# Differential attention with one transpose each for queries and keys, one square sum per half head, and the combination of the softmaxes put ahead of the next row maxima

## The chip, the cores and the metric

The kernel runs on one core of a Trainium2 chip. The metric is device time in microseconds (us) of one execution, as the median of several runs. The core has five engines that run side by side, each with its own queue of instructions: TensorE (PE in the profile; its weight loads, PEld, overlap its matmuls), VectorE (DVE), ScalarE (ACT), GpSimd (POOL) and SyncE (SP), which here only issues transfers between DRAM and on-chip memory. Instructions of different engines wait for one another by semaphores; an instruction that waits holds up everything behind it in its own queue.

## The reference

One decoder layer on 1024 tokens of width 1024: RMSNorm, one input projection, three branches (a chunkwise mLSTM, a causal differential attention, a cross-attention into 256 memory tokens), sigmoid gates, a projection, then a squared-ReLU MLP. The change touches the differential attention alone. It has 8 heads; each has two queries and two keys of width 64 (components 0 and 1) and one value of width 128:

```python
q = rms_norm(q, q_g)
k = rms_norm(k, k_g)
...
s = jnp.einsum('bhcqd,bhckd->bhcqk', qblk, kt).astype(jnp.float32) * scale
s = jnp.where(kpos[None, :] <= qpos[:, None], s, -jnp.inf)
p = jax.nn.softmax(s, axis=-1)
a = p[:, :, 0] - lam * p[:, :, 1]
return jnp.einsum('bhqk,bhkv->bhqv', a.astype(vt.dtype), vt)
```

All arithmetic is float32. The kernel feeds TensorE with a rounded format and so keeps each operand as a high part (the rounded value) and a low part (the rest), and multiplies high by high, high by low and low by high.

## The kernel before, in words

The stages run one after the other: the norm and cross-attention, the mLSTM, a stretch of gate matmuls, the differential attention (`branch_d`) with the remaining gate matmuls as filling, the gates that are still left, the merge (`tail`) and the MLP (`mlp`).

Inside `branch_d` the generator `d_gemm` projects the tokens. A half head (j, 0 to 15) is 512 tokens of one head, in four tiles of 128. A tile takes eight groups of three matmuls (`mm3`), and each `yield` hands control back after one group; `fill(n)` runs n groups, and gate matmuls once the projection is through. When a tile is done, `evict` copies it out of PSUM: the value v as high and low part (dv), the raw queries and keys (draw), and their squares (dscr). `rest`, which `after()` runs at the start of the next step, sums the squares, and for the fourth tile takes the inverse root on POOL (drr) and sets up `prep`, the list of evictions of this half head: `turns` gives transposes of draw (into a PSUM tile that the profile calls pr, the projection's other buffer), queries as qT (dq) and keys as kd and kl (dk, dkl: high and low part).

Before the change draw holds each 64-wide query or key twice side by side. A transpose of 128 x 128 then gives one component with two copies, one above the other on the partitions. In qT one copy stays the high part and the other becomes the low part, so that one matmul of depth 128 against the doubled kd gives high by high and low by high at once; a second matmul against kl adds the rest. Four groups of four transposes serve a half head, one group per step, each with its eviction; the scaling of the keys by their norm (`scale`) stands at the end of the second of these steps.

After eight tiles ahead of it, the main loop runs 64 steps (and five to drain). Step s is one block of 128 queries of head s // 8; its width is 128 x (s % 8 + 1) keys. "Step 0" to "step 7" below means s % 8. A step does, in this order: the scores of component 0 into sc, their row maxima with the mask (the custom VectorE instruction, `tmask`) and the exponential (dpe); `after()`; `combine(s - 1)`, which puts the two exponentials of the step before together; four groups of filling; `values(s - 2)`, the product with v (po) and its two-instruction eviction into doS, a high part on ScalarE and a low part on VectorE; the next entry of `prep`; a group; scores of component 1; the transposes of the combined rows (tp) into daT, high part on ScalarE and low part on VectorE, around the second exponential; three more groups; the second function of the `prep` entry; in between `norm`, in four parts, once in four steps. `ahead` splits the next head's projection weights (w) and asks for the ones after.

While this stage runs, `self.pinned` and `InOrder` make TensorE, VectorE and ScalarE keep the order in which the program was written. SP's queue and POOL's are ordered by the scheduler. Two score tiles, two projection tiles and two tp/po tiles exist in PSUM, and each is reused when its last reader is done.

## Time and profile before

| | |
|---|---|
| median of 3 runs | 2195.02 us (2193.86 to 2195.88) |
| the profiled execution | 2194.59 us, its span 2192.8 us, granted TensorE clock 0.999 |
| main loop's scores on TensorE | first at 646.8 us, last at 1122.6 us |
| transposes of draw (pr) | 256, first at 630.6 us, last at 1086.5 us |
| one head (eight steps) | 59.43 us from 819.82 to 879.25 |

An execution's own time is a little longer than its span. A group of the profile gives line, engine, operation, `written<-read`, then count and durations; in brackets stands the idle time of that engine just before and what ended it. All instructions of the three pinned engines have the line of the helper that records them (67, 92, 95), so the tile names tell them apart. In the table by stretches a row holds the length, then the busy time of PE, PEld, DVE, ACT and POOL with counts, the granted clock, and the transfers' share and rate.

### The profile page before, as it was taken

The numbers are of one execution on the slowest core, as the hardware profiler recorded it, in microseconds if no ns is written. First come the engines' busy times: TensorE is split into PE (matmuls) and PEld (weight loads), VectorE is DVE, ScalarE is ACT, GpSimd is POOL, SyncE is SP. The second block draws the span as 40 slices with busy tenths as digits, with TensorE's granted clock in tenths as the row PEclk, the third lists the DMA queues.
The fourth block names the chain that finished last, engine by engine and source line by source line (L and its number), as shares of the span: only waits on it lengthen the run. The fifth ranks groups of instructions, "written<-read, shape, count | busy, mean of one in ns | idle before, by whom it ended". The sixth has DMA issues, their size and how long they took to land.

```text
span 2192.8 us, 30563 instructions
## 1 busy us (share of the span) xinstructions
PE 2166.7 (99%) x11254; PEld 1874.8 (85%) x11254; DVE 1385.5 (63%) x2628; ACT 969.5 (44%) x1949; POOL 534.9 (24%) x709
## 2 busy tenths in 40 slices
PE   8999999999999999999999999999999999999998
PEld 6888789888899999999888888888878888788887
DVE  6455457554138888888753233454588778876678
ACT  7543445444246666666543111223433333543331
POOL 3210000000011111111100002101566667564444
PEclk9999999999999999999999999999999999999999
DMA  7032222201311111110135344435534454744442
GB/s 252 21 117 87 88 62 79 79 14 63 116 49 35 35 31 39 39 37 25 54 120 173 116 139 130 144 111 177 191 126 159 154 198 158 268 165 158 159 158 96
DMA packets 110947, 242.38 MB, mean 111 GB/s; under 512 B 10921, under 2 KB 19406, under 8 KB 108750
## 3 DMA queue, kind: packets, MB, share of 16 engines
q1 hardware_dynamic: 108494, 227.85, 31.4%
q10 hardware_dynamic: 2304, 12.58, 1.4%
q8 instruction: 88, 1.44, 0.3%
q14 instruction: 61, 0.50, 0.1%
HBM read 173.25 MB, written 67.14 MB: 110 GB/s over the span
## 4 chain that ended last, share of the span: by engine, by line
PE 77%; DVE 12%; ACT 4%; DMA 4%; issue 2%; POOL 1%; SPq 0%; ACTq 0%; POOLq 0%; DVEq 0%
PE mm L92 46%; PE p L92 21%; PE sc L92 4%; PE tp L95 2%; PE po L92 2%; DVE sc L67 1%; ACT dpe L67 1%; DVE dpe L67 1%; DMA raw<-in_wkv 1%; DVE wo L67 1%; DVE draw L67 1%; PE pr L95 1%; DVE dst L67 1%; DVE u L67 1%; POOL wraw L67 1%
## 5 line engine op out<-in xcount | busy, mean ns | idle before, releaser
L92 PE MATMUL mm<-hT,w 128*128 128x512 f32 x1920 | 464.2, 395 | 1.6 <-ACT gt L605 1.6
L92 PE MATMUL mm<-w,hT 128*128 128x384 f32 (+3 forms) x2496 | 454.6, 329 | 0.0
L92 PEld LDWEIGHTS mm<-hT,w 128*128 128x128 f32 x1920 | 353.5, 188 | 75.5 <-ACT gt L605 2.0
L92 PEld LDWEIGHTS mm<-w,hT 128*128 128x128 f32 x2496 | 388.2, 188 | 8.8
L67 POOL TENSOR_TENSOR wraw<-wraw 128x128 f32<-128x128 f32 x496 | 321.3, 672 | 171.3 <-DMA wraw<-in_wdown 127.6
L92 PE MATMUL p<-xo,wo 128*128 128x512 f32 x1344 | 307.6, 390 | 2.2 <-ACT u L67 0.7
L92 PE MATMUL p<-xd,wo 128*128 128x512 f32 x1344 | 305.7, 389 | 0.6 <-DVE acc L67 0.5
L92 PEld LDWEIGHTS p<-xo,wo 128*128 128x128 f32 x1344 | 251.3, 188 | 57.1 <-DVE u L67 2.3
L92 PEld LDWEIGHTS p<-xd,wo 128*128 128x128 f32 x1344 | 252.0, 188 | 54.1 <-DVE acc L67 1.0
L92 PE MATMUL mm<-kt,w 128*128 128x512 f32 x1152 | 261.3, 389 | 0.0
L92 PEld LDWEIGHTS mm<-kt,w 128*128 128x128 f32 x1152 | 216.3, 188 | 44.8
L67 ACT CAST wo<-wraw 128x896 fp32r<-128x896 f32 x125 | 116.5, 944 | 258.1 <-POOL wraw L67 119.7
L67 DVE TENSOR_TENSOR wo<-wraw,wo 128x896 fp32r<-128x896 f32 x125 | 155.7, 1254 | 111.6 <-ACT wo L67 109.6
L67 ACT ACTIVATE dpe<-sc,dst,drr 128x256 f32<-128x256 f32 (+7 forms) x128 | 106.7, 833 | 62.0 <-DVE dst L67 51.9
L116 ACT CAST w<-raw 128x256 fp32r<-128x256 f32 (+2 forms) x128 | 69.0, 567 | 126.6 <-PE mm L92 99.5
L117 DVE TENSOR_TENSOR w<-raw,w 128x256 fp32r<-128x256 f32 (+2 forms) x128 | 81.5, 664 | 41.7 <-ACT w L116 41.7
L67 DVE CUSTOM_DVE_ANT_0 sc<-sc,tmask 128x256 f32<-128x256 f32 (+7 forms) x128 | 96.9, 757 | 3.6 <-PE sc L92 2.4
L140 POOL TENSOR_SCALAR hss<-hss 128x4 f32<-128x4 f32 x8 | 3.5, 442 | 378.0 <-ACT mscr L907 378.0
L92 PE MATMUL mm<-mh,w 128*128 128x512 f32 x256 | 78.9, 389 | 0.0
L106 DVE TENSOR_TENSOR w<-raw,w 128x256 fp32r<-128x256 f32 (+1 forms) x64 | 27.1, 439 | 80.0 <-ACT w L105 79.4
L67 DVE TENSOR_TENSOR w<-raw,w 128x384 fp32r<-128x384 f32 (+2 forms) x112 | 65.8, 598 | 15.8 <-ACT w L67 15.6
L92 PEld LDWEIGHTS po<-dv,daT 128*128 128x128 f32 x576 | 74.8, 189 | 0.9
(325 smaller groups left out, 2947.2 us busy)
## 6 DMA issues: line engine op xcount, KB each, us to landing
wraw<-in_wup SPq DMA_DIRECT2D x64, 256.0 KB, 3.2
r_d<-xts SPq DMA_DIRECT2D x16, 1024.0 KB, 4.2
xd<-r_d SPq DMA_DIRECT2D x16, 1024.0 KB, 5.4
wraw<-in_wdown SPq DMA_DIRECT2D x64, 256.0 KB, 4.2
raw<-in_wgate SPq DMA_DIRECT2D x48, 256.0 KB, 3.1
gates<-gt SPq DMA_DIRECT2D x48, 256.0 KB, 2.1
raw<-in_wd SPq DMA_DIRECT2D x32, 384.0 KB, 3.1
kraw<-y SPq DMA_DIRECT2D x24, 512.0 KB, 4.6
```

The costliest lines, as they stand in the source:

```text
L67: return self.tc.keep_in_program_order(f(*a, **k))
L92: self.pin(self.nc.tensor.matmul(out, l, r, start=start, stop=stop))
L95: self.pin(self.nc.tensor.transpose(out, x, self.ident))
L106: low = lambda: self.V.tensor_sub(lo, src, f32(hi))
L116: nc.scalar.copy(hi, src)
L117: nc.vector.tensor_sub(lo, src, f32(hi))
L140: g.tensor_scalar(r, ss, 1.0 / width, EPS, op0=ALU.mult, op1=ALU.add)
```

## The change

Queries and keys: draw is one tile per half head, without doubling. One group of four transposes turns both queries of four token tiles, a second both keys; component 0 then lies on partitions 0 to 63 and component 1 on 64 to 127. The high parts are copied there, 64 partitions at a time. The query's low part goes to the other 64 partitions of the same component. The key's high part is brought to the other 64 partitions by two transfers from on-chip memory to on-chip memory on SP's queue (`twice`). The key's low part stays where it is, in one of four fixed tiles whose other half POOL fills with zero once. `prep` has three entries: queries with the key scaling behind them, keys, the transfers.

Square sum: one reduction over the four tiles of a half head in place of four; the squares of the four tiles have one tile.

Order: `scores` gives back the row maxima as a function (`top`). For component 0, `combine(s - 1)` now stands ahead of it, and `after()` behind the exponential. In the eight tiles ahead of the loop the first entry of `prep` comes two groups earlier.

On VectorE in step 7, from its first row maxima (ISA is the custom instruction) to the second, before:

```order
L67 ISA sc_9377,dst_9376<-sc_9377,tmask 128x1024
L67 ISA dst_9376 128x1
L67 SCALAR_TENSOR_TENSOR dst_9376<-dst_9376,drr_8363 128x1
L67 TENSOR_REDUCE drr_9107<-dscr_9372 128x4
L67 RECIPROCAL dst_9282<-dst_9282 128x2
L67 SCALAR_TENSOR_TENSOR dst_9282<-dst_9282,dv 128x1
L67 SCALAR_TENSOR_TENSOR dpe_9280<-dpe_9281,dst_9282,dpe_9280 128x896
L67 SCALAR_TENSOR_TENSOR doS_9323<-po_9402,dst_9187,doS_9323 128x128
L67 TENSOR_TENSOR doS_8965<-doS_8965,dso_9295 128x512
L67 TENSOR_TENSOR dkl_9103<-pr_9418,dk_9102 128x512
L67 ISA sc_9428,dst_9376<-sc_9428,tmask 128x1024
```

and now, from the combination:

```order
L67 RECIPROCAL dst_8412<-dst_8412 128x2
L67 SCALAR_TENSOR_TENSOR dst_8412<-dst_8412,dv 128x1
L67 SCALAR_TENSOR_TENSOR dpe_8410<-dpe_8411,dst_8412,dpe_8410 128x896
L67 ISA sc_8499,dst_8498<-sc_8499,tmask 128x1024
L67 ISA dst_8498 128x1
L67 SCALAR_TENSOR_TENSOR dst_8498<-dst_8498,drr_7537 128x1
L67 SCALAR_TENSOR_TENSOR doS_8452<-po_8523,dst_8322,doS_8452 128x128
L67 TENSOR_TENSOR doS_8115<-doS_8115,dso_8424 128x512
L67 ISA sc_8542,dst_8498<-sc_8542,tmask 128x1024
```

The combination (dpe) moved from behind the maxima to ahead of them; the square sum and the key's low part left this step; the low part of the value (doS) now follows the maxima at once.

On ScalarE in step 4, from the first exponential (dpe) to the second, before:

```order
L67 ACTIVATE dpe_9087,dst_9089<-sc_9090,dst_9089,drr_8363 128x640
L67 ACTIVATE doS_8965<-po_9121,dst_8934 128x128
L67 ACTIVATE dq_9101<-pr_9130,dv 128x512
L67 ACTIVATE yd_9145<-tp_9140,dv 128x512
L67 CAST daT_9160<-tp_9155 128x512
L67 CAST w_9164<-raw_8988 128x384
L67 ACTIVATE dpe_9088,dst_9089<-sc_9148,dst_9089,drr_8363 128x640
```

and now:

```order
L67 ACTIVATE dpe_8220,dst_8222<-sc_8223,dst_8222,drr_7537 128x640
L67 ACTIVATE doS_8115<-po_8255,dst_8085 128x128
L67 ACTIVATE dq_8237<-pr_8264,dv 64x512 x2
L67 ACTIVATE yd_8281<-tp_8276,dv 128x512
L67 CAST daT_8296<-tp_8291 128x512
L67 CAST w_8300<-raw_8133 128x384
L67 ACTIVATE dpe_8221,dst_8222<-sc_8284,dst_8222,drr_7537 128x640
```

Both query copies (dq), each 64 high, stand in this step where one stood; step 5 holds both key copies in the same way. The place of the exponential ahead of the value's high part (doS) is the old one.

On SP in the same stretch, weight loads (raw), an output store (y), before:

```order
L1018 DMA raw_8244<-in_wd 128x768
L1018 DMA raw_8418<-in_wd 128x768
L436 DMA y<-yd_8401 128x512
L1018 DMA raw_8698<-in_wd 128x768
L1018 DMA raw_8810<-in_wd 128x768
```

and now:

```order
L1018 DMA raw_8133<-in_wd 128x768
L1018 DMA raw_8298<-in_wd 128x768
L436 DMA y<-yd_8281 128x512
L1083 DMA dk_8238<-dk_8238 64x512 x2
L1018 DMA raw_8556<-in_wd 128x768
L1018 DMA raw_8669<-in_wd 128x768
```

The two doubling transfers (dk) stand behind the store of step 0 or 4 and ahead of the next weight loads.

The diff:

```diff
--- before.py
+++ after.py
@@ -1039,66 +1039,76 @@
         nc = self.nc
         V, A = self.V, self.A
         self.after, self.prep = [], []
-
-        def turns(raws, rr, vh):
+        kls = [pool.tile([P, 2, 512], F32R, tag=f"dkl{i}", name=f"dkl{i}") for i in range(4)]
+        for t in kls:
+            nc.gpsimd.memset(f32(t[64:128, 0]), 0.0)
+            nc.gpsimd.memset(f32(t[0:64, 1]), 0.0)
+
+        def turns(rw, rr, vh, j):
 
             qT = pool.tile([P, 2, 512], F32R, tag="dq", name=self.name("dq"))
             kd = pool.tile([P, 2, 512], F32R, tag="dk", name=self.name("dk"))
-            kl = pool.tile([P, 2, 512], F32R, tag="dkl", name=self.name("dkl"))
+            kl = kls[j % 4]
+            own = (slice(0, 64), slice(64, 128))
 
             def turn(c):
                 pt = self.other_tile()
                 for i in range(4):
-                    self.transpose(pt[:, i * P : (i + 1) * P], raws[i][:, c].rearrange("p a d -> p (a d)"))
+                    self.transpose(pt[:, i * P : (i + 1) * P], rw[:, i, 2 * c : 2 * c + 2].rearrange("p a d -> p (a d)"))
                 return pt
 
-            def q_(c):
-                lo = slice(64 - c * 64, 128 - c * 64)
-                pt = turn(c)
-                A.activation(qT[:, c], pt, AF.Copy, scale=self.gd)
-                V.scalar_tensor_tensor(
-                    out=qT[lo, c], in0=pt[lo], scalar=self.gd[lo], in1=f32(qT[lo, c]), op0=ALU.mult, op1=ALU.subtract
-                )
+            def q_():
+                pt = turn(0)
+                for c in range(2):
+                    A.activation(qT[own[c], c], pt[own[c]], AF.Copy, scale=self.gd[own[c]])
+                for c in range(2):
+                    V.scalar_tensor_tensor(
+                        out=qT[own[1 - c], c], in0=pt[own[c]], scalar=self.gd[own[c]], in1=f32(qT[own[c], c]),
+                        op0=ALU.mult, op1=ALU.subtract,
+                    )
 
             def scale():
-                for i in range(4):
-                    k_ = raws[i][:, 2:4].rearrange("p c a d -> p c (a d)")
-                    V.tensor_mul(k_, k_, rr[:, i, 2:4].unsqueeze(2).broadcast_to([P, 2, P]))
-
-            def k_(c):
-                pt = turn(2 + c)
-                A.copy(kd[:, c], pt)
-                V.tensor_sub(kl[:, c], pt, f32(kd[:, c]))
-                if c == 1:
-                    kv.append((qT, kd, kl, vh, rr))
+                k_ = rw[:, :, 2:4]
+                V.tensor_mul(k_, k_, rr[:, :, 2:4].unsqueeze(3).broadcast_to([P, 4, 2, 64]))
+
+            def k_():
+                pt = turn(1)
+                for c in range(2):
+                    A.copy(kd[own[c], c], pt[own[c]])
+                for c in range(2):
+                    V.tensor_sub(kl[own[c], c], pt[own[c]], f32(kd[own[c], c]))
+
+            def twice():
+                for c in range(2):
+                    nc.sync.dma_start(f32(kd[own[1 - c], c]), f32(kd[own[c], c]))
+                kv.append((qT, kd, kl, vh, rr))
 
             none = lambda: None
-            return [(lambda: q_(0), none), (lambda: q_(1), scale), (lambda: k_(0), none), (lambda: k_(1), none)]
-
-        def evict(ps, i, raws, vh, rr):
+            return [(q_, scale), (k_, none), (twice, none)]
+
+        def evict(ps, i, rw, scr, vh, rr, j):
             v = pool.tile([P, 2, P], F32R, tag="dv", name=self.name("dv"))
             self.split2(v[:, 0], v[:, 1], ps[:, 256:384])
-            rw = pool.tile([P, 4, 2, 64], F32, tag="draw", name=self.name("draw"))
-            A.copy(rw, ps[:, 0:256].rearrange("p (a d) -> p a d", a=4).unsqueeze(2).broadcast_to([P, 4, 2, 64]))
-            scr = pool.tile([P, 256], F32, tag="dscr", name=self.name("dscr"))
-            A.activation(scr, ps[:, 0:256], AF.Square)
-            raws.append(rw)
+            A.copy(rw[:, i], ps[:, 0:256].rearrange("p (a d) -> p a d", a=4))
+            A.activation(scr[:, i], ps[:, 0:256], AF.Square)
             vh.append(v)
 
             def rest():
-                V.tensor_reduce(rr[:, i], scr.rearrange("p (a d) -> p a d", a=4), axis=AX.X, op=ALU.add)
-                if i == 3:
-                    rl = rr.rearrange("p a b -> p (a b)")
-                    self.rsqrt_mean(rl, rl, 64, 16)
-                    self.prep = turns(raws, rr, vh)
-
-            self.after.append(rest)
+                rl = rr.rearrange("p a b -> p (a b)")
+                V.tensor_reduce(rl, scr.rearrange("p i (a d) -> p (i a) d", a=4), axis=AX.X, op=ALU.add)
+                self.rsqrt_mean(rl, rl, 64, 16)
+                self.prep = turns(rw, rr, vh, j)
+
+            if i == 3:
+                self.after.append(rest)
 
         for j in range(16):
             hd, hf = divmod(j, 2)
             w = self.dw[hd]
             rr = pool.tile([P, 4, 4], F32, tag="drr", name=self.name("drr"))
-            vh, raws = [], []
+            rw = pool.tile([P, 4, 4, 64], F32, tag="draw", name=self.name("draw"))
+            scr = pool.tile([P, 4, 256], F32, tag="dscr", name=self.name("dscr"))
+            vh = []
             for i in range(4):
                 s = slice((hf * 4 + i) * P, (hf * 4 + i + 1) * P)
                 ps = self.mm_tile(384)
@@ -1106,7 +1116,7 @@
                     self.mm3(ps, (self.hT[:, k, 0, s], self.hT[:, k, 1, s]), w[k], k == 0, k == NK - 1)
                     if k < NK - 1:
                         yield True
-                evict(ps, i, raws, vh, rr)
+                evict(ps, i, rw, scr, vh, rr, j)
                 yield True
 
     def branch_d(self, pool, dw):
@@ -1160,14 +1170,16 @@
                 o = sc[:, h2 * 512 : h2 * 512 + w_]
                 self.mm(o, q_, kv[hd * 2 + h2][1][:, c, 0:w_], start=True, stop=False)
                 self.mm(o, q_, kv[hd * 2 + h2][2][:, c, 0:w_], start=False, stop=True)
-            V.tensor_tensor_reduce(
-                out=sc[:, 0:n], in0=sc[:, 0:n], in1=self.tmask[:, D - n : D], scale=1.0, scalar=-3.0e38,
-                op0=ALU.add, op1=ALU.max, accum_out=t8[:, c : c + 1],
-            )
-            V.scalar_tensor_tensor(
-                out=t8[:, 2 + c : 3 + c], in0=t8[:, c : c + 1], scalar=-1.0, in1=rr[:, i, c : c + 1],
-                op0=ALU.mult, op1=ALU.mult,
-            )
+
+            def top():
+                V.tensor_tensor_reduce(
+                    out=sc[:, 0:n], in0=sc[:, 0:n], in1=self.tmask[:, D - n : D], scale=1.0, scalar=-3.0e38,
+                    op0=ALU.add, op1=ALU.max, accum_out=t8[:, c : c + 1],
+                )
+                V.scalar_tensor_tensor(
+                    out=t8[:, 2 + c : 3 + c], in0=t8[:, c : c + 1], scalar=-1.0, in1=rr[:, i, c : c + 1],
+                    op0=ALU.mult, op1=ALU.mult,
+                )
 
             def exp():
                 A.activation(
@@ -1175,7 +1187,7 @@
                     accum_out=t8[:, 4 + c : 5 + c],
                 )
 
-            return exp
+            return top, exp
 
         def combine(s):
 
@@ -1254,11 +1266,11 @@
         for n in range(8):
             fill(1)
             after()
-            fill(3)
+            fill(1)
             p = self.prep.pop(0) if self.prep else None
             if p:
                 p[0]()
-            fill(2)
+            fill(4)
             ahead(n)
             fill(2)
             if p:
@@ -1267,10 +1279,13 @@
             hh, i = divmod(s - 2, 4)
             more = s < NS
             if more:
-                scores(s, 0)()
-            after()
+                top, exp = scores(s, 0)
             if 1 <= s <= NS:
                 combine(s - 1)
+            if more:
+                top()
+                exp()
+            after()
             if hh >= 1 and i == 0:
                 norm(hh - 1, 1)
             fill(4)
@@ -1285,7 +1300,8 @@
             if hh >= 1 and i == 2:
                 norm(hh - 1, 3)
             if more:
-                exp = scores(s, 1)
+                top, exp = scores(s, 1)
+                top()
             self.defer = []
             if 1 <= s <= NS:
                 hi, lo = turn(s - 1, 0)
@@ -1882,7 +1898,7 @@
                             next(self.gates)
                             if n - 64 in (3, 7, 11, 15, 19, 23, 26, 30):
                                 next(dw)
-                    with tc.tile_pool(name="pd", bufs=2) as pd, tc.tile_pool(name="pd3", bufs=3) as pd3, tc.tile_pool(name="pdm", bufs=1) as pdm, tc.tile_pool(name="pd5", bufs=7) as pd5, tc.tile_pool(name="pdv", bufs=5) as pdv, tc.tile_pool(name="pdv2", bufs=17) as pdv2, tc.tile_pool(name="pd4", bufs=4) as pd4:
+                    with tc.tile_pool(name="pd", bufs=2) as pd, tc.tile_pool(name="pd3", bufs=3) as pd3, tc.tile_pool(name="pdm", bufs=1) as pdm, tc.tile_pool(name="pd5", bufs=2) as pd5, tc.tile_pool(name="pdv", bufs=5) as pdv, tc.tile_pool(name="pdv2", bufs=17) as pdv2, tc.tile_pool(name="pd4", bufs=4) as pd4:
                         self.tmask = ptm.tile([P, D], F32, name="tmask")
                         nc.gpsimd.memset(self.tmask, 0.0)
                         nc.gpsimd.affine_select(
@@ -1892,7 +1908,7 @@
                         class T4:
                             def tile(_, shape, dt, tag, name):
                                 tag = "dscr2" if tag == "gt" else tag
-                                p = pd5 if tag == "draw" else pdv if tag == "drr" else pdv2 if tag == "dv" else pd4 if tag in ("dk", "dkl") else pdm if tag == "dpe1" else pd3 if tag in ("daT", "dst") else pdm if tag in ("dscr", "dscr2", "y") else pd
+                                p = pd5 if tag == "draw" else pdv if tag == "drr" else pdv2 if tag == "dv" else pd4 if tag == "dk" else pdm if tag.startswith("dkl") else pdm if tag == "dpe1" else pd3 if tag in ("daT", "dst") else pdm if tag in ("dscr", "dscr2", "y") else pd
                                 return p.tile(shape, dt, tag=tag, name=name)
                         self.gpool = T4()
                         self.branch_d(T4(), dw)
```

## Prediction

> **What bounds the kernel now.** I read the page first, then the stage's time by step, then single instructions of one step. The page says that TensorE is never idle for long:
>
> ```profile
> PE 2166.7 (99%) x11254; PEld 1874.8 (85%) x11254; DVE 1385.5 (63%) x2628; ACT 969.5 (44%) x1949; POOL 534.9 (24%) x709
> ```
>
> That is a mean over stages, so I cut one head (eight steps, width 128 to 1024) at the starts of its steps on TensorE. A row is a step: its length, then busy time of PE, PEld, DVE, ACT, POOL.
>
> ```profile
> 819.82:828.18 8.36, 8.11 (x59) 7.89 (x58) 7.37 (x19) 6.69 (x16) 3.10 (x2) 1.00 0.25 79
> 828.18:835.20 7.02, 7.02 (x51) 7.02 (x50) 4.37 (x16) 3.64 (x11) 0.00 (x0) 1.00 0.00 0
> 835.20:841.37 6.17, 5.96 (x38) 5.64 (x38) 5.79 (x18) 4.37 (x12) 1.14 (x2) 1.00 0.25 66
> 841.37:847.68 6.31, 6.31 (x41) 6.10 (x40) 5.81 (x20) 4.30 (x11) 0.07 (x1) 1.00 0.00 0
> 847.68:855.17 7.49, 7.49 (x51) 7.27 (x51) 6.45 (x17) 5.98 (x13) 3.10 (x2) 1.00 0.28 88
> 855.17:862.61 7.44, 7.44 (x50) 7.24 (x50) 6.04 (x16) 5.14 (x12) 0.00 (x0) 1.00 0.01 2
> 862.61:870.62 8.01, 8.01 (x53) 7.77 (x53) 7.61 (x20) 4.85 (x12) 1.21 (x2) 1.00 0.17 50
> 870.62:879.25 8.63, 8.63 (x57) 8.20 (x56) 7.48 (x20) 5.93 (x13) 0.00 (x0) 1.00 0.01 2
> sum 59.43, PE 58.96 PEld 57.13 DVE 50.92 ACT 40.90 POOL 8.61; mean PE 7.37 PEld 7.14 DVE 6.37 ACT 5.11 POOL 1.08
> ```
>
> The reader is to see two things. TensorE idles 59.43 - 58.96 = 0.47 us a head, so it sets the end. But in steps 6 and 7 VectorE is busy 7.61 of 8.01 and 7.48 of 8.63. How near it is to taking over, its own rows of step 7 tell (start, duration):
>
> ```profile
> 873.04 1.22 DVE L67 CUSTOM_DVE_ANT_0 sc<-sc,tmask 128x1024 f32<-128x1024 f32 x1
> ...
> 874.36 0.16 DVE L67 SCALAR_TENSOR_TENSOR dst<-dst,drr 128x1 f32<-128x1 f32 x1
> 874.44 0.41 DVE L67 TENSOR_REDUCE drr<-dscr 128x4 f32<-128x256 f32 x1
> 874.77 0.15 DVE L67 RECIPROCAL dst<-dst 128x2 f32<-128x2 f32 x1
> ...
> 875.21 1.15 DVE L67 SCALAR_TENSOR_TENSOR dpe<-dpe,dst,dpe 128x896 f32<-128x896 f32 x1
> 876.28 0.34 DVE L67 SCALAR_TENSOR_TENSOR doS<-po,dst,doS 128x128 f32<-128x128 f32 x1
> 876.54 0.68 DVE L67 TENSOR_TENSOR doS<-doS,dso 128x512 f32<-128x512 f32 x1
> 877.14 0.68 DVE L67 TENSOR_TENSOR dkl<-pr,dk 128x512 fp32r<-128x512 f32 x1
> 877.74 1.22 DVE L67 CUSTOM_DVE_ANT_0 sc<-sc,tmask 128x1024 f32<-128x1024 f32 x1
> ...
> 881.01 0.56 DVE L67 TENSOR_TENSOR daT<-tp,daT 128x384 fp32r<-128x384 f32 x1 [0.26 <-ACT daT L67]
> ...
> 881.68 0.29 DVE L67 CUSTOM_DVE_ANT_0 sc<-sc,tmask 128x128 f32<-128x128 f32 x1
> ```
>
> From first row maxima to the next step's first row maxima VectorE takes 881.68 - 873.04 = 8.64 us, with one short wait, against TensorE's 8.63. Here both engines bind together. And ScalarE's rows of the same step:
>
> ```profile
> 874.64 1.21 ACT L67 ACTIVATE dpe<-sc,dst,drr 128x1024 f32<-128x1024 f32 x1 [0.60 <-DVE dst L67]
> ...
> 875.83 0.36 ACT L67 ACTIVATE doS<-po,dst 128x128 f32<-128x128 f32 x1
> ...
> 879.31 1.21 ACT L67 ACTIVATE dpe<-sc,dst,drr 128x1024 f32<-128x1024 f32 x1 [0.37 <-DVE dst L67]
> ...
> 880.51 0.47 ACT L67 CAST daT<-tp 128x384 fp32r<-128x384 f32 x1
> 880.87 0.28 ACT L67 CAST dv<-mm 128x128 fp32r<-128x128 f32 x1
> ```
>
> The first exponential runs from 874.64 to 875.83, and just then VectorE is at the square sum and the combination (874.44 to 876.28). The combination hides the exponential. That cover is what the change takes away.
>
> **The transposes.** The chain of waits in the eight tiles ahead of the loop prices them:
>
> ```profile
> 630.72 0.44 PE pr L95 x4
> 631.15 4.19 PE mm L92 x24
> ```
>
> Four transposes take 0.44 us of TensorE's time and 24 matmuls 4.19 (12 of them 2.10). Sixteen half heads each lose two of their four groups: 32 x 0.44 = 14.1 us of TensorE's work. In the loop the groups vanish from steps 2, 3, 6 and 7, so TensorE's own need per head is 58.96 - 4 x 0.44 = 57.2 us.
>
> **The order on VectorE.** After the change each step runs: combination, first maxima, (square sum), value low part, evictions, second maxima, low parts. The value low part (doS) waits for ScalarE's value high part, which is queued behind the first exponential. Nothing long stands on VectorE in between any more. So the step becomes one file of work that alternates between two engines. For step 7, from the rows above, start to start: combination with its two small instructions 876.28 - 874.77 = 1.51; first maxima to exponential 874.64 - 873.04 = 1.60; exponential 1.19; value high part 0.36 and 0.03 of handover (880.51 + 0.47 to 881.01) 0.39; value low part 0.26; norm product 0.60; second maxima to exponential 879.31 - 877.74 = 1.57, taken as 1.60; exponential 1.19; copy to low part 0.50; low part to next step 881.68 - 881.01 = 0.67. Sum 9.51, although the key's low part and the square sum have gone from this step. TensorE needs 8.63 - 0.44 = 8.19.
>
> The other steps follow by width. These rows give duration min/median/max in ns, from width 128 to 1024 for the first three, 128 to 512 for daT (the third row's maximum lies outside the head shown; I use 1.15 at 896 from above):
>
> ```profile
> L67 DVE CUSTOM_DVE_ANT_0 sc<-sc,tmask x128: 289/758/1233, 647.7 to 1123.1; 128x128 f32<-128x128 f32 x16, 128x256 f32<-128x256 f32 x16, 128x384 f32<-128x384 f32 x16, 128x512 f32<-128x512 f32 x16
> L67 ACT ACTIVATE dpe<-sc,dst,drr x128: 457/832/1213, 648.6 to 1124.7; 128x128 f32<-128x128 f32 x16, 128x256 f32<-128x256 f32 x16, 128x384 f32<-128x384 f32 x16, 128x512 f32<-128x512 f32 x16
> L67 DVE SCALAR_TENSOR_TENSOR dpe<-dpe,dst,dpe x64: 350/832/1572, 654.8 to 1127.6; 128x128 f32<-128x128 f32 x8, 128x256 f32<-128x256 f32 x8, 128x384 f32<-128x384 f32 x8, 128x512 f32<-128x512 f32 x8
> L67 ACT CAST daT<-tp x96: 252/529/591, 655.9 to 1133.0; 128x512 fp32r<-128x512 f32 x48, 128x128 fp32r<-128x128 f32 x16, 128x256 fp32r<-128x256 f32 x16, 128x384 fp32r<-128x384 f32 x16
> L67 DVE TENSOR_TENSOR daT<-tp,daT x96: 282/620/694, 657.0 to 1133.6; 128x512 fp32r<-128x512 f32 x48, 128x128 fp32r<-128x128 f32 x16, 128x256 fp32r<-128x256 f32 x16, 128x384 fp32r<-128x384 f32 x16
> L67 ACT ACTIVATE dq<-pr,dv x32: 687/687/689, 631.2 to 1072.3; 128x512 fp32r<-128x512 f32 x32
> L67 DVE SCALAR_TENSOR_TENSOR dq<-pr,dv,dq x32: 742/750/759, 631.9 to 1073.0; 64x512 fp32r<-64x512 f32 x32
> L67 ACT CAST dk<-pr x32: 580/584/589, 640.4 to 1087.4; 128x512 fp32r<-128x512 f32 x32
> L67 DVE TENSOR_TENSOR dkl<-pr,dk x32: 677/683/692, 641.1 to 1088.5; 128x512 fp32r<-128x512 f32 x32
> ```
>
> Per 128 columns the maxima cost 0.135, the exponential 0.108, the combination 0.133 more. Maxima to exponential is the duration plus 0.37 (step 7); the combination is the duration less an overlap of 0.08, plus 0.44.
>
> **Evictions.** Both halves are now evicted in one step: queries in steps 0 and 4, keys in 1 and 5. After the exponential: value high part 0.26, two query copies 0.69 + 0.59, handover 0.03, two low parts 0.75 + 0.62, together 2.94; for keys 0.26 + 1.10 + 1.20 = 2.56. I take a height of 64 at the same time as 128, since the 64-high query row is already no shorter than its neighbours. Both low parts stand behind both copies in the recorded order.
>
> **Sums.** Combination + (maxima, exponential) + middle + (maxima, exponential) + rest. Step 0: 1.64 + 1.12 + 2.94 + 1.12 + 2.03 = 8.85. Step 1: 0.71 + 1.35 + 2.56 + 1.35 + 0.49 = 6.46. Step 2: 0.84 + 1.60 + 0.65 + 1.60 + 0.49 = 5.18. Step 3: 0.98 + 1.84 + 1.25 + 1.84 + 0.49 = 6.40. Step 4: 1.11 + 2.09 + 2.94 + 2.09 + 1.09 = 9.32. Step 5: 1.24 + 2.33 + 2.56 + 2.33 + 0.68 = 9.14. Step 6: 1.38 + 2.57 + 0.65 + 2.57 + 0.93 = 8.10. Step 7: 9.51. The rest is the last transposed copy and low part by width, the token values (0.28, then 0.20), and in steps 0 and 4 the key scaling (0.60, as a 512-wide product). Together 62.96 us a head, against 57.2 for TensorE and 59.43 now. TensorE may run ahead by about 3 us (scores 0.9 and 12 matmuls 2.1 before it needs the previous step's low parts), and steps 1 and 2, where the file is shorter than TensorE's step, win back only 0.9, so from the first wide steps on the file sets the pace.
>
> **The rest of the edit.** One square sum for four tiles costs 0.41 (one now) to 1.64 (four); it lies under the first exponential and the query copies either way: 0. POOL's root takes 3.10 us after it; the scaling stands at the step's end, some 5 us later, also 0. If that cover went, 1 us at most, twice a head. ScalarE's copy is half as wide and its VectorE cover longer: 0. The zero fills are on POOL, idle then: 0. The doubling copies join SP's queue:
>
> ```profile
> y<-yd SPq DMA_DIRECT2D x16, 256.0 KB, 2.0
> lamv<-in_lamv SPq DMA_DIRECT2D x1, 128.0 KB, 10.8
> raw<-in_wd SPq DMA_DIRECT2D x32, 384.0 KB, 3.1
> ```
>
> The first two rows bound 128 KB by 2.0 and 10.8 us. What stands ahead of the copies on SP belongs to the same or earlier steps, they are issued at the latest in step 2 or 6, and the scores need them two steps on, 11.4 us (5.52 + 5.87, steps 2 and 3 shortened): I take 0. The weight loads queued behind them land in 3.1 us and are split two steps after they are asked for, so that also hides.
>
> **The sum.** The file rules from step 4 of the first head to the end of the seventh: six heads and four steps. 6 x 62.96 + 36.07 = 413.8, where TensorE now takes 6 x 59.43 + 31.57 = 388.2: +25.6. Of this TensorE's run ahead takes off once 3.0 - 0.8 = 2.2. Two groups before the loop and two in steps 2 and 3 of the first head save 4 x 0.44 = 1.8; in the last head, where wider gate matmuls fill TensorE and no tiles are left to evict, two groups save 0.9. +25.6 - 2.2 - 1.8 - 0.9 = +20.7 on the profiled execution's 2194.59 (0.43 under the median): 2215. Each step's sum may be off by 0.15, so a head by 1.2 and the total by 8: own range 2207 to 2223.
>
> **Rivals.** First, TensorE goes on setting the end: the lag never outgrows its 3 us, and the work removed comes off. 14.1 and seven heads' idle time of 0.47, 3.3: 2177. For it speaks PE 58.96 of 59.43; against it, that VectorE already has no slack in step 7, and that 5.8 of the 62.96 would have to be wrong (3.5 for no loss). [...]
>
> Second, the low parts start as soon as their own copy is done, not after both: 0.59 and 0.49, twice a head, 2.2 x 6.5 = 14 less, 2201. For it: the copies are separate instructions; against it, both write one tile and the second low part carries no wait of its own.
>
> Third, the doubled keys come late: it decides only beyond 11 us, above the larger row, and then costs its excess sixteen times, 2 us late giving 2247.
>
> **Chances.** Forecast 0.75, first rival 0.13, second 0.10, third 0.02. About 0.2% (4.4 us) is what can be told from no change. Faster is the first rival and a little of what lies between, 0.14; the low end of the second, under 2199, makes same 0.06; slower 0.80. The range 2194 to 2226 takes in the forecast and the second rival; the first and the third stay out.
>
> **What would show it.** Right: a head of about 63 us between like steps; VectorE idle about 1 us before doS in steps 6 and 7, released by ScalarE; TensorE waiting on daT, doS or the low parts in steps 5 to 0; its busy time down by 14 us. Transposes right alone: 128 pr matmuls instead of 256. Wrong: a head of 57 to 58 us, or no VectorE wait for doS; then the first rival holds. PE waiting on a DMA of dk would be the third.

## The result and the profile after

The changed kernel takes 2227.48 us (median of 4 runs, 2226.43 to 2230.16), the kernel before beside it 2194.44 (2192.71 to 2195.88): ratio 1.0153, 95% interval 1.0135 to 1.017. It is slower by 33 us. The forecast was 2215, so the direction came out and the size was 12 us short, 1.5 us above the range's top. The profiled execution took 2227.12 us, with a span of 2225.2.

Part 1 of the page after, busy time by engine:

```profile
PE 2170.9 (98%) x11126; PEld 1867.6 (84%) x11126; DVE 1369.3 (62%) x2532; ACT 949.7 (43%) x1949; POOL 536.3 (24%) x717
```

There are 128 matmuls fewer, yet TensorE is not less busy (2166.7 before): the fall by 14 us that the prediction named as a sign did not come. The last section comes back to this. The stage by step tells more. These rows cut one head of the changed kernel at VectorE's first row maxima (length, then busy PE, PEld, DVE, ACT, POOL, granted clock):

```profile
837.63:845.78 8.15, 7.81 (x55) 7.34 (x55) 7.04 (x20) 5.49 (x14) 3.10 (x2) 1.00 0.10 35
845.78:852.81 7.03, 7.02 (x48) 6.74 (x47) 4.70 (x17) 4.28 (x13) 0.00 (x0) 1.00 0.24 45
852.81:858.08 5.27, 5.27 (x33) 5.15 (x32) 4.33 (x16) 3.71 (x11) 1.21 (x2) 1.00 0.18 66
858.08:864.56 6.48, 6.48 (x43) 6.27 (x41) 4.86 (x15) 3.60 (x10) 0.00 (x0) 1.00 0.10 9
864.56:874.23 9.67, 9.06 (x61) 8.68 (x61) 8.12 (x18) 5.85 (x13) 3.10 (x2) 1.00 0.16 63
874.23:883.84 9.61, 8.32 (x50) 7.49 (x50) 6.89 (x18) 5.97 (x14) 0.00 (x0) 1.00 0.22 48
883.84:892.02 8.18, 6.32 (x28) 5.59 (x27) 6.06 (x16) 4.20 (x10) 1.21 (x2) 0.79 0.07 25
892.02:901.88 9.86, 9.86 (x69) 9.61 (x68) 7.59 (x18) 5.36 (x12) 0.00 (x0) 1.00 0.14 41
sum 64.25, PE 60.15 PEld 56.87 DVE 49.61 ACT 38.47 POOL 8.62; mean PE 7.52 PEld 7.11 DVE 6.20 ACT 4.81 POOL 1.08
```

A head is 64.25 us instead of 59.43. TensorE, which before lost 0.47 us a head, now stands still above all in steps 4, 5 and 6 (0.61, 1.29 and 1.86 us). What it waits for, VectorE's rows of step 7 tell:

```profile
890.95 1.15 DVE L67 SCALAR_TENSOR_TENSOR dpe<-dpe,dst,dpe 128x896 f32<-128x896 f32 x1
892.02 1.23 DVE L67 CUSTOM_DVE_ANT_0 sc<-sc,tmask 128x1024 f32<-128x1024 f32 x1
893.34 0.16 DVE L67 SCALAR_TENSOR_TENSOR dst<-dst,drr 128x1 f32<-128x1 f32 x1
895.20 0.35 DVE L67 SCALAR_TENSOR_TENSOR doS<-po,dst,doS 128x128 f32<-128x128 f32 x1 [1.70 <-ACT doS L67]
895.47 0.68 DVE L67 TENSOR_TENSOR doS<-doS,dso 128x512 f32<-128x512 f32 x1
896.11 1.23 DVE L67 CUSTOM_DVE_ANT_0 sc<-sc,tmask 128x1024 f32<-128x1024 f32 x1
```

ScalarE's rows of the same step:

```profile
893.61 1.21 ACT L67 ACTIVATE dpe<-sc,dst,drr 128x1024 f32<-128x1024 f32 x1 [2.33 <-DVE dst L67]
894.81 0.36 ACT L67 ACTIVATE doS<-po,dst 128x128 f32<-128x128 f32 x1
```

This is the file that was forecast: the combination at 890.95 holds up the maxima, ScalarE stands idle 2.33 us until they are there, and then VectorE stands idle 1.70 us through the whole first exponential, because the value high part is queued behind it. The waits from 640 to 1180 us (us in total, times, longest), after:

```profile
ACT dpe L67 <- DVE dst L67: 151.0, 113, 2.9
DVE doS L67 <- ACT doS L67: 55.3, 52, 3.4
PEld tp L95 <- DVE doS L67: 37.2, 28, 2.2
PE tp L95 <- DVE doS L67: 29.9, 25, 1.9
```

and before:

```profile
ACT dpe L67 <- DVE dst L67: 51.9, 74, 1.4
DVE doS L67 <- ACT doS L67: 22.7, 20, 3.4
PEld tp L95 <- DVE doS L67: 2.7, 7, 0.4
```

The last rows are how the file reaches TensorE: the value's product (po) and the transposes (tp) share a ring of two buffers, and VectorE's value low part is the last reader of po. When it is late, TensorE's next transpose waits (29.9 us in all after).

### The profile page after: what moved, and what is told of

Its sections match the earlier page's. It is cut to its first block, busy times and chain, and to the rows that moved or that the text cites. A ratio compares the mean times of both kernels' runs of the same rounds, so it can differ in the third digit from the quotient of the medians.

```text
span 2225.2 us, 30331 instructions
## 1 busy us (share of the span) xinstructions
PE 2170.9 (98%) x11126; PEld 1867.6 (84%) x11126; DVE 1369.3 (62%) x2532; ACT 949.7 (43%) x1949; POOL 536.3 (24%) x717
## 4 chain that ended last, share of the span: by engine, by line
PE 51%; DVE 11%; ACT 7%; issue 1%; DMA 1%; POOL 0%; ACTq 0%; POOLq 0%; DVEq 0%; SPq 0%
PE p L92 24%; PE mm L92 23%; ACT dpe L67 4%; DVE sc L67 3%; DVE dst L67 2%; DVE dpe L67 2%; PE sc L92 1%; DVE dkl L67 1%; PE po L92 1%; DVE doS L67 1%; PE tp L95 1%; ACT dk L67 1%; ACT doS L67 1%; DVE dq L67 1%; ACT dq L67 1%
## 5 line engine op out<-in xcount | busy, mean ns | idle before, releaser
L92 PE MATMUL mm<-w,hT 128*128 128x384 f32 (+3 forms) x2496 | 459.8, 331 | 1.8 <-DVE dkl L67 1.1
L95 PE MATMUL tp<-ident,dpe 128*128 128x128 f32 x288 | 49.5, 281 | 32.1 <-DVE doS L67 29.9
```

Source lines behind the costliest of these rows:

```text
L92: self.pin(self.nc.tensor.matmul(out, l, r, start=start, stop=stop))
L95: self.pin(self.nc.tensor.transpose(out, x, self.ident))
```

## Experiments

Each row gives the steps 0 to 7 of the fourth head, from the start of VectorE's first row maxima to the next step's, then the head's length and the median time. The kernel before, run beside each group, took 2192.1 to 2192.9 us.

| kernel | 0 | 1 | 2 | 3 | 4 | 5 | 6 | 7 | head | us |
|---|---|---|---|---|---|---|---|---|---|---|
| before | 6.89 | 8.34 | 5.41 | 6.11 | 7.08 | 9.08 | 7.88 | 8.64 | 59.43 | 2194.4 |
| changed | 8.15 | 7.03 | 5.27 | 6.48 | 9.67 | 9.61 | 8.18 | 9.86 | 64.25 | 2227.5 |
| e1 order undone | 8.65 | 7.16 | 4.57 | 5.73 | 9.36 | 8.23 | 6.96 | 8.25 | 58.91 | 2189.1 |
| e2 order alone | 6.14 | 8.42 | 6.08 | 7.08 | 7.67 | 9.64 | 9.00 | 10.23 | 64.26 | 2227.3 |
| e3 low part late | 9.41 | 8.11 | 4.64 | 5.55 | 9.67 | 10.66 | 9.76 | 9.58 | 67.38 | 2257.1 |
| e4 tiles split | 8.14 | 7.03 | 5.27 | 6.48 | 9.67 | 9.61 | 8.18 | 9.63 | 64.01 | 2226.3 |
| e6 pair late, old order | 8.47 | 6.49 | 5.05 | 6.03 | 9.38 | 7.16 | 6.96 | 8.71 | 58.25 | 2184.6 |
| e7 pair late, new order | 7.50 | 6.80 | 5.26 | 6.49 | 9.10 | 8.36 | 8.18 | 9.64 | 61.33 | 2205.8 |
| e8 both late | 8.92 | 7.25 | 5.16 | 6.04 | 9.88 | 8.04 | 7.72 | 9.57 | 62.58 | 2217.2 |
| e9 value first | 7.93 | 7.38 | 4.63 | 5.68 | 10.17 | 9.33 | 7.09 | 8.30 | 60.51 | 2202.1 |
| e10 e7 and e9 | 7.37 | 6.95 | 5.16 | 6.16 | 9.51 | 7.77 | 7.10 | 8.84 | 58.86 | 2188.6 |

**Which part costs: the order undone (e1), and the order alone (e2).** e1 against the changed kernel:

```diff
-            if 1 <= s <= NS:
-                combine(s - 1)
             if more:
                 top()
                 exp()
             after()
+            if 1 <= s <= NS:
+                combine(s - 1)
```

> The changed kernel with only the order on VectorE put back: first row maxima and first exponential first, then the combination; the paired transposes and evictions and the one square sum stay. Theory (the order is what costs): the combination hides the first exponential again, the file of work per head falls to about 58 us by the step rows, under or at TensorE's need of 57.2, so 2177 to 2190 us, a ratio to the kernel before of 0.992 to 0.998; the wait of ScalarE's exponential for the row maxima falls from 151 us to about the 52 us of before. Rival (the paired evictions are what costs, since both low parts stand behind both copies): the time stays near the changed kernel's, above 2210.

e2 against the kernel before (`scores` returns `top` and `exp` apart, as in the changed kernel):

```diff
             if more:
-                scores(s, 0)()
-            after()
+                top, exp = scores(s, 0)
             if 1 <= s <= NS:
                 combine(s - 1)
+            if more:
+                top()
+                exp()
+            after()
```

> The kernel before with only the order changed: combination ahead of the first row maxima; four separate transposes per half head, single evictions and a square sum per tile as before. Theory (order): the file of work per head is about 63.3 us by the step rows against TensorE's 59.0, so about 2218 us (2212 to 2226), ratio 1.008 to 1.014, with a wait of ScalarE's exponential for row maxima well over 100 us. Rival (paired evictions cost): near the kernel before, 2190 to 2200.

e1: 2189.11 us, ratio 0.9985 (0.9975 to 0.9994). e2: 2227.32, ratio 1.0156 (1.0141 to 1.0171), 1 us above the range expected. The order by itself is the whole loss, and the other edits by themselves are a gain of 3 us that vanishes under the new order. The wait of the exponential for the maxima (640 to 1180 us) in e1 and then in e2:

```profile
ACT dpe L67 <- DVE dst L67: 82.4, 96, 2.0
```

```profile
ACT dpe L67 <- DVE dst L67: 137.8, 112, 2.9
```

In e1 I had expected about 52 us, as before; the paired evictions hold on to some of the wait (37.2 us in e6, which moves them). The head of e2 is 64.26 us where the step rows gave 63.3. Its step 1 takes 8.42 us with VectorE busy 5.61 of them, near the 8.34 of the kernel before, where TensorE is busy all 8.34 us; I take it that TensorE still sets this step, and a sum of files alone misses such a step.

**Where in the file: the value low part later (e3).** The low part (`doS` on VectorE) is returned from `values` as a function and called behind the second `top()`:

```diff
-            V.scalar_tensor_tensor(
+            return lambda: V.scalar_tensor_tensor(
                 out=o[:, i], in0=po[:, 128:256], ...
...
-            if 2 <= s < NS + 2:
-                values(s - 2)
+            late = values(s - 2) if 2 <= s < NS + 2 else lambda: None
...
                 top, exp = scores(s, 1)
                 top()
+            late()
```

> The changed kernel with one thing moved: the value's low part (doS on VectorE) stands behind the second row maxima instead of ahead of them, so that in steps without evictions VectorE goes from the first to the second row maxima without waiting for the first exponential. Theory (the step is one file of work through exponential and value parts): steps 2, 3, 6 and 7 lose their wait for doS, 2 to 2.4 us a head, about 2212 us (2207 to 2218); VectorE's wait at doS falls from 55 us to under 25; steps 0, 1, 4 and 5 keep their length. Rival (the file is set elsewhere, by the evictions or by TensorE's waits for buffers): within 4 us of the changed kernel, or slower, since TensorE gets the value's buffer back later.

2257.12 us, ratio 1.0291 (1.0268 to 1.0313): a miss, to the wrong side. Steps 2 and 3 did get 0.6 and 0.9 us shorter, but steps 0 and 1 got 1.3 and 1.1 longer, and steps 5 and 6 longer too. Part of these last two is, I take it, the clock: the head in the table holds a stretch of TensorE's slower clock (granted 0.65 on the mean from 888 to 892 us; last section), and the next head has 10.15 and 8.73 there and takes 65.82 us. Three of the six equal heads take 67.35 to 67.38 us, the other three 65.65 to 65.82; if the clock is the difference, it makes some 5 of the 30 us (an estimate, 3 x 1.56). VectorE's rows of step 5:

```profile
885.45 1.39 DVE L67 TENSOR_TENSOR dkl<-pr,dk 64x512 fp32r<-64x512 f32 x2 [2.56 <-ACT dk L67]
886.87 0.97 DVE L67 CUSTOM_DVE_ANT_0 sc<-sc,tmask 128x768 f32<-128x768 f32 x1
888.05 0.34 DVE L67 SCALAR_TENSOR_TENSOR doS<-po,dst,doS 128x128 f32<-128x128 f32 x1
```

TensorE's row there:

```profile
888.54 0.30 PE L95 MATMUL tp<-ident,dpe 128*128 128x128 f32 x1 [3.55 <-DVE doS L67]
```

The low part now stands behind the key pair and the second maxima, po is kept so long, and TensorE stands still 3.55 us. My expectation had named this rival.

**Do the two halves of a pair wait for each other by their tile (e4).** Queries and keys of each half get tiles of their own; instructions and order stay. The lines that use them, and the low parts' tiles, change to match and are left out here.

```diff
-            qT = pool.tile([P, 2, 512], F32R, tag="dq", name=self.name("dq"))
-            kd = pool.tile([P, 2, 512], F32R, tag="dk", name=self.name("dk"))
+            qT = [pool.tile([P, 512], F32R, tag=f"dq{c}", name=self.name("dq")) for c in range(2)]
+            kd = [pool.tile([P, 512], F32R, tag=f"dk{c}", name=self.name("dk")) for c in range(2)]
```

> The changed kernel with the two halves of the queries and of the keys in tiles of their own instead of one tile each: the same instructions in the same order, but the first low part waits for the first copy alone and no longer for both. My sum took both low parts to stand behind both copies, and the trace shows 0.91 us of wait ahead of the pair. If that wait is part of the file: about 0.7 us less in each of steps 0, 1, 4 and 5, 2.8 us a head, about 2208 us (2204 to 2214), with the steps 0 and 4 at about 8.9 to 9.0 and 1 and 5 at about 7 and 8.9. Rival (TensorE or another wait ends last there): 2222 to 2230.

2226.33 us, ratio 1.0153 (1.0138 to 1.0168): no change, and the reason is that the wait did not go away. ScalarE's pair of e4, then VectorE's:

```profile
866.34 1.37 ACT L67 ACTIVATE dq<-pr,dv 64x512 fp32r<-64x512 f32 x2
```

```profile
867.74 1.51 DVE L67 SCALAR_TENSOR_TENSOR dq<-pr,dv,dq 64x512 fp32r<-64x512 f32 x2 [0.92 <-ACT dq L67]
```

Both low parts still start after both copies: what they share besides the tile is the transposes' buffer (pr), which ScalarE and VectorE both read. So e4 says only that the destination is not what ties them. Giving each half a buffer of its own was not tried.

**The pair out of the file (e6, e7).** `q_` and `k_` return their two low parts as one function, called behind the second `top()`: in e6 on top of e1, in e7 on top of the changed kernel.

```diff
-            if p:
-                p[0]()
+            pair = p[0]() if p else None
...
                 top()
+            if pair:
+                pair()
```

> The kernel with the old order on VectorE (first row maxima ahead of the combination) and the paired transposes, in which both low parts of a pair of evictions stand behind the second row maxima instead of ahead of them. With the old order alone put back the head was 58.93 us, of which TensorE was busy 57.88 (98.2%); its longest steps against TensorE's need were those with pairs (9.36 in step 4). Theory (the pair, which has VectorE wait for two copies and then does two low parts before the second row maxima, is what still keeps TensorE waiting): head 57.6 to 58.2 us, time 2180 to 2185 us, ratio 0.994 to 0.997. Rival (TensorE then waits for the transposes' buffer, which comes free some 1.5 us later): 2188 us or more.

> The changed kernel, its order kept, with both low parts of a pair behind the second row maxima. Theory (the step is one file of work between VectorE and ScalarE, and everything that stands between the first and the second row maxima lengthens it): the second row maxima no longer wait for the pair's copies, steps 0 and 4 lose about 1.2 us (then ScalarE's queue of copies sets the second exponential), 1 and 5 about 1.4 us, 5.2 us a head, so about 58.8 to 59.5 a head and 2193 us (2188 to 2203); the steps 2, 3, 6 and 7 stay at 5.27, 6.48, 8.18 and 9.64. Rival (the value's low part and its buffer, not the evictions, hold the steps): 2215 us or more, with TensorE still waiting over 40 us for that buffer.

e6: 2184.62 us, ratio 0.9959 (0.9946 to 0.9973), better than both kernels. One of its heads:

```profile
817.25:875.50 58.25, 57.66 (x374) 55.62 (x374) 49.39 (x126) 39.36 (x96) 8.61 (x8) 1.00 0.16 46
```

TensorE is busy 57.66 of 58.25, nearly all the time as before, so this is close to what the paired transposes can give.

e7: 2205.76, ratio 1.0054 (1.004 to 1.0068), 22 us better than the changed kernel and 3 us above the range I expected. Steps 2, 3, 6 and 7 stayed within 0.01 us (7 as in heads without the slower clock, below), and step 5 lost 1.25. Steps 0 and 4 lost only 0.6, not 1.2, and step 1 only 0.2; TensorE had been busy through all of that step, which I take to be the reason.

**Is it the buffer that e3 lost by (e8).** e7 with the value low part behind the second maxima, ahead of the pair (`late` as in e3).

```diff
                 top()
+            late()
             if pair:
                 pair()
```

> The changed kernel's order with the pair's low parts behind the second row maxima, and the value's low part moved behind them too, just ahead of the pair. The value's low part alone moved had cost 30 us, with TensorE waiting up to 3.6 us for the value's buffer in step 5, where the pair stood ahead of it. Theory (that loss was the buffer kept through the pair's copies and low parts; the gain in the steps without pairs, where VectorE no longer waits for the first exponential, was real): steps 2 and 3 about 4.6 and 5.6 us, 6 and 7 about 1 us shorter than 8.18 and 9.64, the head near TensorE's 58.2, time 2184 to 2194. Rival (the value's buffer, given back later, costs TensorE as much as VectorE gains, also without the pair): 2202 or more.

2217.18 us, ratio 1.0112 (1.0094 to 1.013): the rival. Without the pair ahead of it the late low part costs 11 us against e7, not 30. Steps 6 and 7 gained 0.5 and 0.1 instead of 1, and steps 0, 1 and 4 lost 1.4, 0.5 and 0.8. In this run VectorE waits for scores:

```profile
DVE sc L67 <- PE sc L92: 79.5, 61, 2.7
```

The second maxima need scores that TensorE makes late. Ahead of its transposes TensorE stands still for the value low part (17.4 us from 640 to 1180 us, 11.1 in e7) and for ScalarE's copy of a finished output, yd (10.1 us from 700 to 1060 us, 2.0 in e7). That these waits are what makes the scores late is not shown, and what of the loss is the buffer I could not split.

**The exponential's place in ScalarE's queue (e9, e10).** The first `exp()` is called behind `values(s - 2)`, so that ScalarE does the value high part first; VectorE's order is untouched. e9 does it to the changed kernel, e10 to e7.

```diff
                 top()
-                exp()
             after()
...
                 values(s - 2)
+            if more:
+                exp()
```

> The changed kernel with one thing moved on ScalarE: the value's high part stands ahead of the first exponential instead of behind it, so that VectorE's low part of it no longer waits for the exponential. VectorE's order is untouched. Theory (with the combination ahead of the maxima nothing covers the first exponential, and the low part's wait for it is what makes the step a file): VectorE's wait at the value's low part falls from 55 us to under 25, step 7 from 9.64 to about 8.4, step 6 from 8.18 to about 7.4, the steps with pairs by 0 to 0.3 each, since the pair's copies still stand behind the exponential; head about 61.5, time 2206 to 2214. Rival (the pair's evictions alone are what is left to gain): 2222 or more, with steps 6 and 7 as they were.

> The changed kernel's order with both: the value's high part ahead of the first exponential and the pair's low parts behind the second row maxima. Theory: nothing on VectorE between the first and the second row maxima waits for the first exponential any more, the head falls to what TensorE needs, 58.2 us, and the time to 2183 to 2190, a ratio of 0.995 to 0.998. Rival (the combination at the head of the step still delays the row maxima, so that exponentials come too late whatever stands behind): 2195 or more.

e9: 2202.13 us, ratio 1.0044 (1.0029 to 1.0059). One swap on ScalarE takes back 25 of the 33 us and ends 4 us below the range expected. VectorE in step 7:

```profile
818.75 1.23 DVE L67 CUSTOM_DVE_ANT_0 sc<-sc,tmask 128x1024 f32<-128x1024 f32 x1
820.07 0.16 DVE L67 SCALAR_TENSOR_TENSOR dst<-dst,drr 128x1 f32<-128x1 f32 x1
820.18 0.35 DVE L67 SCALAR_TENSOR_TENSOR doS<-po,dst,doS 128x128 f32<-128x128 f32 x1
820.45 0.68 DVE L67 TENSOR_TENSOR doS<-doS,dso 128x512 f32<-128x512 f32 x1
821.26 1.23 DVE L67 CUSTOM_DVE_ANT_0 sc<-sc,tmask 128x1024 f32<-128x1024 f32 x1
```

From first to second maxima it is 2.51 us instead of 4.09, and no wait stands in it; the exponential (1.21) now runs under the value low part and the second maxima. Over the stage the wait of TensorE's transposes for the low part falls with VectorE's own (29.9 to 5.4 us), so e9 does not tell the two apart. Steps 6 and 7 are near what I expected, 7.09 and 8.30. Step 4 became longer, 10.17, not shorter. ScalarE's row there:

```profile
854.34 0.37 ACT L67 ACTIVATE doS<-po,dst 128x128 f32<-128x128 f32 x1 [2.02 <-PE po L92]
```

The value high part waits for TensorE's product, and now the exponential waits behind it: it starts 1.95 us after the first maxima do, in the changed kernel 1.19, and the pair's copies follow it. TensorE is busy all 10.17 us of that step.

e10: 2188.57 us, ratio 0.9981 (0.9972 to 0.9991). With both cures the new order no longer loses against the kernel before, and the head is 58.86 us with TensorE busy 58.03 of it. It is not better than the old order with the same late pair, 2184.6 in e6.

## Why the prediction was right and where it was wrong

**Held.** The loss comes from the order (e1, e2), by the uncovered first exponential (e9) and by what stands between the two maxima (e7). The sums of the steps without pairs were right: from maxima to maxima my figures for steps 2, 3, 6 and 7 are 5.32, 6.53, 8.23 and 9.64, measured 5.27, 6.48, 8.18, and 9.64 in heads at full clock. VectorE's wait for doS, "about 1 us" by the prediction, was 1.00 in step 6 and 1.70 in step 7. The key scaling takes the 0.60 that the sum gives it (872.38 to 872.98 in step 4). The square sum and the doubled keys cost nothing that the trace shows: the row for the keys answers the third rival, and no instruction waits for them.

```profile
dk<-dk SPq DMA_DIRECT2D x30, 128.0 KB, 2.2
```

**Failed: the terms for pairs.** I gave two copies 1.28 us (queries) and 1.10 (keys) and two low parts 1.37 and 1.20, as if the second of a pair started early. In the changed kernel the instructions of one pair do not overlap: two query copies of 0.68 us take 1.37, their low parts of 0.75 take 1.51, the key copies of 0.58 take 1.18 and their low parts of 0.69 take 1.39. The query copies and low parts of step 4, then the key copies and low parts of step 5:

```profile
866.88 1.37 ACT L67 ACTIVATE dq<-pr,dv 64x512 fp32r<-64x512 f32 x2
868.28 1.51 DVE L67 SCALAR_TENSOR_TENSOR dq<-pr,dv,dq 64x512 fp32r<-64x512 f32 x2 [0.91 <-ACT dq L67]
876.79 1.18 ACT L67 CAST dk<-pr 64x512 fp32r<-64x512 f32 x2
878.00 1.39 DVE L67 TENSOR_TENSOR dkl<-pr,dk 64x512 fp32r<-64x512 f32 x2 [0.72 <-ACT dk L67]
```

From ScalarE's value high part to VectorE's second maxima this makes 3.20 us for my 2.94 (866.63 to 869.83), and 2.88 for my 2.56 (876.54 to 879.42). Steps 0, 4 and 5 came out 0.23, 0.22 and 0.33 above my 7.92, 9.45 and 9.28. Step 1 is 0.44 above 6.59; the same stretch is 2.97 for 2.56 there, and TensorE is busy 7.02 of 7.03. Together this makes 64.0 us a head instead of 62.96, 6.4 us over six heads; three of them have a step 7 longer by 0.22 (below), which makes 7.1.

**Failed: that the file rules from step 4 of the first head, less 2.2 us of TensorE's run ahead.** The stage cut at the first head's steps 0 to 3, 4 to 7, and the six heads after. Before:

```profile
647.68:670.61 22.93, 22.70 (x142) 22.02 (x141) 17.92 (x59) 15.37 (x41) 3.11 (x2) 1.00 0.13 35
670.61:703.35 32.74, 32.74 (x214) 31.79 (x213) 28.61 (x71) 22.10 (x48) 4.30 (x4) 1.00 0.09 25
703.35:1059.95 356.60, 353.83 (x2327) 342.47 (x2326) 304.59 (x818) 244.60 (x576) 51.69 (x48) 1.00 0.12 35
```

After:

```profile
646.28:672.05 25.77, 24.18 (x145) 23.14 (x144) 18.02 (x56) 15.09 (x43) 3.11 (x2) 1.00 0.15 38
672.05:709.14 37.09, 33.54 (x214) 31.14 (x213) 28.61 (x64) 20.90 (x48) 4.31 (x4) 1.00 0.13 37
709.14:1094.01 384.87, 357.11 (x2219) 336.73 (x2218) 296.37 (x745) 229.98 (x576) 51.70 (x48) 0.98 0.14 40
```

The first head is longer by 2.84 + 4.35 = 7.2 us, where I had 36.07 - 31.57 - 2.2 - 0.9 = 1.4. The file rules from the first steps on: steps 0 to 3 grew by 2.84 us, where I had them 0.9 shorter. TensorE's being ahead shortened nothing of steps 4 to 7, which are as long (37.09) as in a later head at full clock (37.11). These 5.8 us, the 7.1 in the six heads (28.27 against 21.2), and -1.3 at the two ends (-1.40 and -1.66 against -0.9 twice) make, rounded, the 11.7 by which +20.7 fell short of the spans' +32.4.

**Rivals.** The first asked TensorE to set the end; it comes close to that in e6, busy 57.66 of 58.25, and there at 2184.6, not 2177. A group of transposes is worth less in the loop than the 0.44 us of the tiles ahead of it. The kernel before on TensorE (start, duration):

```profile
844.31 0.62 PE L95 MATMUL pr<-ident,draw 128*128 128x128 f32 x4
844.69 0.78 PE L92 MATMUL mm<-w,hT 128*128 128x384 f32 x3
```

That is 0.38 from start to start. TensorE had 128 matmuls fewer and the time rose by 33 us, since the two engines that feed it had become one file. With the old order and the late pair (e6) the time did fall, by 8 us. The second rival did not come: in the changed kernel, as in e4, both low parts wait for both copies. The one tile that I gave as the reason is not what ties them, since e4 gives each half its own.

## What to carry to other kernels

When two engines hand work to and fro, look at what runs under each long instruction and ask what covers it after a reorder; here a combination of 1.5 us hid an exponential of 1.2, and moving it made a step of both. Then look at the other engine's queue: putting the short instruction that others wait for ahead of the long one took back 25 of the 33 us without touching the order, though undoing the order took back all of it. Before moving a last read later, ask whose buffer it frees: the same low part that made VectorE wait made TensorE wait longer when it was put off.

## What the runs showed of the hardware

In this stage of the changed kernel TensorE's granted clock fell to 0.50 after four stalls of 1.85 to 1.86 us. One of these waits ends at 887.18, and from 888.51 on the granted clock (third number from a row's end) is half. The stretch in pieces:

```profile
888.00:888.50 0.50, 0.50 (x4) 0.50 (x3) 0.47 (x4) 0.02 (x1) 0.00 (x0) 1.00 0.00 0
888.50:889.00 0.50, 0.50 (x4) 0.41 (x3) 0.49 (x1) 0.50 (x1) 0.00 (x0) 0.51 0.00 0
...
891.50:892.00 0.50, 0.50 (x3) 0.50 (x3) 0.50 (x1) 0.00 (x0) 0.00 (x0) 0.57 0.00 0
892.00:892.50 0.50, 0.50 (x5) 0.50 (x4) 0.50 (x2) 0.00 (x0) 0.00 (x0) 1.00 0.00 0
```

It lasts 3.413 us (888.51 to 891.92), and a score matmul takes 0.62 us there instead of 0.39. Such a stretch, each time 3.413 us long, follows this stall in four of the six equal heads, the first three and the sixth. The four starts, at 758.81, 823.66, 888.51 and 1079.66, lie 64.85, 64.85 and 191.15 us apart, in this trace whole multiples (19, 19 and 56) of the measured length. In the 3.41 us ahead of each of them TensorE is idle for 1.85 to 1.86 us. In the other two heads the same stall of 1.86 us, to 951.42 and to 1015.44, is followed by no slow stretch, and the clock stays at 1.00; counted on from 888.51 in pieces of 3.413 us, it falls across two pieces there, with 1.47 and 1.22 us of idle time in the fuller one. What brings the slow clock on these runs do not show.

The cost is small here, 0.22 us in step 7 of the first three (9.86 and 9.64); in e3 the head with a slow stretch is 1.56 us longer than the next. Slow matmuls count as busy (0.49 of 0.49 us from 888.51 to 889.00, at clock 0.50), but they are a small part of why the page's busy time did not fall with the work: TensorE is busy 60.15 us in the fourth head, 59.77 in the fifth without the slow clock, and 58.96 before. In e2, which has the matmuls of before and a clock of 0.998 over the whole run, it is some 60.4 of 64.26 (an estimate: TensorE's waits from 700 to 1060 us, 18.4 for doS and 3.1 for dscr, come to 3.8 a head). What else counts as busy when TensorE has to wait stays open.

In e4 VectorE's first low part needs, by the program, only the first of ScalarE's two query copies, which take 0.68 us each and run from 866.34 to 867.71. It starts at 867.74, after the second has ended, having stood idle 0.92 us. Both engines read the transposes' buffer (pr) there, and nothing else passes between the second copy and this low part; what makes it wait no run shows.
